# A 64-row score matmul of latent attention, given 128 rows by a zeroed upper half

## The chip, the cores and the metric

The kernel runs on one core of a Trainium2 chip. The metric is the device time of one execution in microseconds (us), the lower the better. Times are medians of several executions. The engines are named as in the profile: PE (TensorE matmul), PEld (TensorE weight load), DVE (VectorE), ACT (ScalarE), POOL (GpSimd) and SP (SyncE, which issues most of the DMAs).

## What is computed

The kernel is one inference step of a two-layer decoder: a prompt of 1024 tokens and 8 new tokens share all weights. Layer 0 mixes with a gated MLP and a convolution, layer 1 with latent attention, and each layer ends in a SwiGLU FFN. The change lies in the prompt's attention in layer 1, which the reference computes so, for each of 8 heads (the nope part of a query or key has 128 features, the rotary part 64, and the rotary key is shared by all heads):

```python
q_nope, q_pe, ckv, kpe = mla_project(h, pos, w_in_c, q_norm, kv_norm, w_uq)
k_nope = jnp.einsum('btr,rhn->bthn', ckv, w_uk)
...
s = (jnp.einsum('bqhn,bkhn->bhqk', qn_b, k_nope)
     + jnp.einsum('bqhp,bkp->bhqk', qp_b, kpe)).astype(jnp.float32) * ATTN_SCALE
...
s = jnp.where(kpos[None, :] <= qpos[:, None], s, -jnp.inf)
p = jax.nn.softmax(s, axis=-1).astype(v.dtype)
return jnp.einsum('bhqk,bkhv->bqhv', p, v)
```

## The kernel before

Everything is float32 in value. For the large products each operand is split into a high and a low part of a type that TensorE multiplies in one pass, and three products are added up in PSUM (high by high, high by low, low by high).

**The rotary part.** The rotary key has 64 features. `KD` (128 rows by 1024 keys) holds the key's high part twice, in rows 0 to 63 and again in rows 64 to 127 (L788, with a DMA at L787 that doubles the rows). `KL` (64 rows) holds the key's low part (L789). The query tile `QS` has 128 rows: the high part of the rotary query above its low part. So the matmul of `QS` with `KD` gives high by high and low by high at once (L1097), and the matmul of the upper 64 rows of `QS` with `KL` gives high by low (L1098).

**The scores.** `scores` (from L1077) goes over the blocks of 128 queries of a chunk; a chunk is three such blocks, or two at the end. Block i sees (i+1) x 128 keys, in pieces of at most 512. A piece is a group of five matmuls into one PSUM tile `mm`: L1094 and L1095 with the stationary `qh`, L1096 with `qlo`, L1097 and L1098 with `QS`. Then DVE adds the mask of the diagonal block (L1100) and takes the maximum (L1101), and ACT takes the exponential (L1103). There are 12 pieces a head and 96 in all: 48 of 512 keys, and 16 each of 128, 256 and 384.

**Work around it.** In each of 24 steps (8 heads by 3 chunks) `weave` mixes the scores of this step with the values of the step before (transposes at L1137, products at L1148 to L1150), the values' preparation (L1047 to L1049) and pieces of the attention of the 8 new tokens (L938, L939, L941, L1001), whose matmuls have outputs of 32 columns and, at L941, 64 rows. The keys of a head are made by `mm3` (L202 to L204) with 512 columns. There are four `mm` and four `aux` tiles in PSUM. The tile framework then fixes one order for each engine; every engine takes its instructions in that order and waits on semaphores. POOL zeroes a mask (L748), issues the DMAs of the rotary key (L785, L787) and, in the attention, gathers the cache pages (L893). SP loads the query tiles (L1075) and the weights (L167).

Of the kernel before, what the change touches and what calls it, by code (L numbers as in the profile page):

```python
# [66 lines left out]

# [1 line left out]
UNITS = []  # L69
# [31 lines left out]

# [1 line left out]
VC = {}  # L103
# [9 lines left out]
def hybrid_step(ctx: ExitStack, tc: tile.TileContext,  # L113
# [11 lines left out]

# [1 line left out]
    ident = const.tile([P, P], F32, name="ident")  # L127
# [28 lines left out]

# [1 line left out]
    WR, WS = 2, 4  # L158
# [35 lines left out]

# [1 line left out]
    class Env:  # L196
# [16 lines left out]
    def auxtile():  # L213
        return env.psum.tile([P, 512], F32, tag="aux", name="aux", bufs=env.naux)
# [21 lines left out]
    def rstd_rows(acc, n, width):  # L236
        """1/sqrt(acc summed over partitions / width + eps), the same on every partition, in PSUM."""
        blocks = [(b, min(P, n - b * P)) for b in range((n + P - 1) // P)]
        pst = auxtile()
        for b, w in blocks:  # L240
            PE.matmul(pst[:w, b:b + 1], acc[:, b * P:b * P + w], ones[:, 0:1], start=True, stop=True)
        r = small()
        full = len([1 for b, w in blocks if w == P])
        ACT.activation(r[:, :full], pst[:, :full], AF.Sqrt, bias=eps_t, scale=1.0 / width)
        if full < len(blocks):
            w = blocks[-1][1]
            ACT.activation(r[:w, full:full + 1], pst[:w, full:full + 1], AF.Sqrt, bias=eps_t[:w], scale=1.0 / width)
        DVE.reciprocal(r[:, :full], r[:, :full])
        if full < len(blocks):
            DVE.reciprocal(r[:w, full:full + 1], r[:w, full:full + 1])  # L250
        dg = tmp()
        for b, w in blocks:
            DVE.tensor_scalar(dg[:w, b * P:b * P + w], ident[:w, :w], r[:w, b:b + 1], None, ALU.mult)
        prs = auxtile()
        for b, w in blocks:
            PE.matmul(prs[:, b * P:b * P + w], ones[:w, :], dg[:w, b * P:b * P + w], start=True, stop=True)  # L256
        return prs
# [10 lines left out]
    def gemm_act(u, c, ps):  # L268
        """128 output features (unit of 8 x 128 columns) x token chunk c."""
        wh, wl = unit(u)  # L270
        c0, n = CH[c]
        for k in range(KT):
            mm3(ps[:, :n], wh[:, k * P:(k + 1) * P], wl[:, k * P:(k + 1) * P],
                ah(k, c0, c0 + n), al(k, c0, c0 + n), k == 0, k == KT - 1)
# [27 lines left out]

    # DRAM scratch
    x_spill = tc.dram_tile([KT, P, T], F32, name="x_spill")
    # scaled queries of every head, in two parts: nope hi, nope lo, rope (hi above lo)
    q_spill = tc.dram_tile([HEADS, 3, P, SEQ], F32, name="q_spill")
# [16 lines left out]

    # ======================= layer 0: even mixer =======================
    with ExitStack() as ph:
# [18 lines left out]

        # w_s[g, 0, 0] times the 8 x 8 identity
        w8 = p1.tile([NB, 4, NB], F32, name="w8")
        for g in range(4):
            DVE.tensor_scalar(w8[:, g, :], ident[:NB, :NB], w00B[:, g:g + 1], None, ALU.mult)

# [1 line left out]
        conv_ops = []  # L351
# [4 lines left out]
        def fma(out, i, a, k, e0, e1):  # L356
            """tap k of channel tile i over the tokens e0..e1-1"""
            r = DVE.scalar_tensor_tensor(out, G[:, i, k + e0:k + e1], cw[:, i, k:k + 1], a[:, e0:e1], ALU.mult, ALU.add)  # L358
            if PIN:
                tc.keep_in_program_order(r)  # L360
# [4 lines left out]
        def conv_early(i0):  # L365
            """the first chunk of tokens, all taps but the last"""
            accs = [cacc(), cacc()]
# [40 lines left out]

# [1 line left out]
        def pair(m, c):  # L410
# [40 lines left out]

# [1 line left out]
        def sample_conv():  # L453
# [17 lines left out]
        if SC == 0:  # L471
            sample_conv()
# [1 line left out]
        NTOK = 9  # L474
# [8 lines left out]
        def v_stats(n, w):  # L483
            """of a tile of tokens: vst[0] = -mean, vst[1] = sum of squares about the mean"""
            mean = vst[:w, 0, n:n + 1]
# [57 lines left out]

# [1 line left out]
        Tbs = {}  # L545
        utiles = {}

        def gate(m, c):
# [3 lines left out]
            if c == 0:  # L552
                Tb = p1.tile([P, P], F32, tag="Tb", name="Tb", bufs=4)
                pr = auxtile()  # row sums of the masked spatial weights, on every partition
                PE.matmul(pr[:, :P], ones, wsT[:, g, :], start=True, stop=True)
                DVE.scalar_tensor_tensor(Tb, pr[:, :P], col("gb", m), bsB[:, g, :], ALU.mult, ALU.add)
                Tbs[m] = Tb
# [39 lines left out]

# [1 line left out]
        def add_x(m, c, ps):  # L599
# [15 lines left out]

# [1 line left out]
        def ln_conv(c):  # L617
# [28 lines left out]

    # ======================= FFN =======================
    def ffn(layer, final):
# [84 lines left out]

    # ======================= layer 1: latent attention =======================
    xstack.close()
# [5 lines left out]
    KD = mp.tile([P, SEQ], F32R, name="KD")  # L741
    KL = mp.tile([64, SEQ], F32R, name="KL")
    qs_n = mp.tile([P, HEADS, NB], F32, name="qs_n")
# [8 lines left out]
    with ExitStack() as ph:  # L752
# [18 lines left out]
        def evac_c(u, c, ps):  # L771
# [7 lines left out]
            else:  # L779
# [8 lines left out]
                ACT.copy(KD[:, c0:c0 + npr], kr[:, :npr])  # L788
                DVE.tensor_tensor(KL[:, c0:c0 + npr], kr[:64, :npr], KD[:64, c0:c0 + npr].bitcast(F32), ALU.subtract)  # L789
                if c == 2:  # L790
# [25 lines left out]

        # queries: tiles 0..7 = nope of a head; 8, 10 = first rope halves of 4 heads; 9, 11 = second halves
        def spill(src, n, hi_to, lo_to, eng):
            """SCALE * src in two parts"""
            th, tl = [env.tmp.tile([P, 512], F32R, tag="t", name="t", bufs=env.ntmp) for _ in range(2)]  # L820
# [44 lines left out]

# [1 line left out]
    acts["pool"].release()  # L867
    with ExitStack() as ph:
# [3 lines left out]
        def sample_attention():  # L872
            """Generator: the attention of the 8 new tokens over their pages, cut into pieces."""
            sp = pa
# [6 lines left out]
            DVE.tensor_copy(idx, pgf[:, :64])  # L881
            # queries in the latent space, 8 heads a token; 32 columns are taken from a token's first one on,
            # and only the first 8 of the rows that come out are used
            ql = sp.tile([P, 2, 88], F32, name="ql")
# [20 lines left out]
            for g in range(4):  # L905
# [10 lines left out]
                if g % 2:  # L916
                    yield
            # the new latent rows, token-major
            cn8 = sp.tile([NB, 256], F32, name="cn8")
# [7 lines left out]
            for r in range(2):  # L927
# [45 lines left out]
                yield  # L973
                # probabilities with the keys on the partitions, then the latent outputs
                ols = sp.tile([P, 256], F32, tag="ols", name="ols", bufs=1)
# [62 lines left out]
        def prep_v(hp):  # L1038
            """values of heads 2hp, 2hp+1, token-major"""
            wh, wl = unit(("uv", hp // 2))  # L1040
# [37 lines left out]
        def scores(h, c, out):  # L1078
            c0, n = CP[c]
            qh, qlo, QS = KQ.pop(("q", h, c))  # L1080
            for i in range(c0 // P, (c0 + n) // P):
# [3 lines left out]
                two = len(pieces) == 2  # L1085
                # -maximum of each piece, sums, factors, then -maximum and 1/sum of the row
                st = pa.tile([P, 8], F32, tag="st", name="st", bufs=6)
                prs = []
                for pi, (a, e) in enumerate(pieces):
# [7 lines left out]
                    PE.matmul(o, QS[:, r], KD[:, a:e], start=False, stop=False, skip_group_check=True)  # L1097
                    PE.matmul(o, QS[:64, r], KL[:, a:e], start=False, stop=True, skip_group_check=True)  # L1098
                    if e == nk:
# [60 lines left out]
        def out_proj_half():  # L1160
            """heads 0..3 through the output projection, added to the residual in DRAM (prompt tokens)"""
            for q in range(4):
# [22 lines left out]
        def weave(gens):  # L1185
            """takes items of several generators in turn, each spread over the whole"""
            lists = gens
# [51 lines left out]
    for c0, n in CH:  # L1239
        for k in range(KT):  # L1240
            (nc.gpsimd if k % 2 < XQ else nc.sync).dma_start(XT[:, k, c0:c0 + n], x_spill[k][:, c0:c0 + n])
# [1 line left out]
    rawp = tc.alloc_tile_pool(name="rawp", bufs=1, reuse_waits="tile")  # L1243
# [38 lines left out]
def _unit_array(u, w):  # L1282
    """One unit of weights, [128 partitions, 1024]: 128 rows of a factor on the partitions."""
    def cols(a, c0, n):
# [125 lines left out]
```

## Time and profile before

| what | value |
|---|---|
| median of 3 executions | 2805.55 us |
| their range | 2802.09 to 2808.86 us |
| span of the profiled execution (first to last instruction) | 2785.5 us |
| PE busy, share of the span | 2732.5 us, 98% |
| PEld busy | 2615.7 us, 94% |
| DVE, ACT, POOL busy | 1437.2, 751.2, 206.7 us |
| granted TensorE clock, mean | 0.993 of full speed |

The profile gives the span of the profiled execution and no total of its own. The median of the three timed executions is 20.05 us above that span; this is what lies around it (the launch and the end). A busy share of 98% on PE counts every matmul from its start to its modelled end, and the ends overlap the next start. What one matmul really takes from the stream is the distance from its start to the start of the next one.

### The profile page before, as it was taken

The page shows a single profiled execution, that of the slowest core. Times are in us where ns is not written, and L with a number is a line of the kernel's source. Part 1 is how long each engine was busy: PE and PEld are TensorE (multiplying, and loading weights), DVE is VectorE, ACT ScalarE, POOL GpSimd, SP SyncE. Part 2 cuts the span into 40 slices and gives each one's busy share as a digit, 9 for nine tenths or more (in the row PEclk, how much of TensorE's full clock was granted, in tenths as well). Part 3 has the DMA queues.
Part 4 walks back from the last instruction along what each step waited for, and adds up shares of the span by engine and source line. Part 5 has one row for each costly group of instructions (what it writes and reads, how often), then busy time and mean ns, then how long its engine had stood idle before and what let it go on. Part 6 is the DMA issues. An engine that isn't in the chain of part 4 may idle for free.

```text
span 2785.5 us, 41891 instructions
## 1 busy us (share of the span) xinstructions
PE 2732.5 (98%) x17434; PEld 2615.7 (94%) x17434; DVE 1437.2 (52%) x2716; ACT 751.2 (27%) x1562; POOL 206.7 (7%) x293
## 2 busy tenths in 40 slices
PE   7999999999999999999997999999999999999998
PEld 7999999999999999999996867967999999999998
DVE  8999889765232323232754557457652323232325
ACT  5112531542212121212342435235422121212122
POOL 0000010000000000000101144243100000000000
PEclk9999999999999999999998999999999999999999
DMA  3111122112111111111313644442211111111111
GB/s 117 62 47 47 48 70 68 60 33 67 46 52 48 46 46 46 46 46 46 115 60 125 227 125 122 157 131 88 100 61 42 50 52 47 46 46 46 46 46 61
DMA packets 79949, 197.29 MB, mean 71 GB/s; under 512 B 11824, under 2 KB 41712, under 8 KB 79760
## 3 DMA queue, kind: packets, MB, share of 16 engines
q1 hardware_dynamic: 64816, 152.85, 16.7%
q0 software_dynamic: 14944, 41.78, 4.8%
q8 instruction: 136, 2.23, 0.3%
q14 instruction: 53, 0.43, 0.0%
HBM read 166.57 MB, written 27.74 MB: 70 GB/s over the span
## 4 chain that ended last, share of the span: by engine, by line
PE 77%; DMA 2%; DVE 1%; ACT 0%; issue 0%; SPq 0%; DVEq 0%; ACTq 0%
PE mm L202 22%; PE mm L204 21%; PE mm L203 21%; DMA q_spill<-t 2%; PE aux L1137 1%; PE mm L1098 1%; PE mm L1094 1%; PE mm L1095 1%; PE aux L938 1%; PE aux L941 1%; PE mm L1148 1%; PE mm L1149 1%; PE mm L1097 1%; PE mm L1096 1%; PE mm L1150 1%; PE aux L256 1%
## 5 line engine op out<-in xcount | busy, mean ns | idle before, releaser
L202 PE MATMUL mm<-act_hia,whi 128*128 128x384 f32 (+2 forms) x1812 | 582.6, 322 | 3.5 <-ACT cz L775 1.3
L204 PE MATMUL mm<-act_hia,wlo 128*128 128x384 f32 (+2 forms) x1812 | 580.2, 321 | 1.0 <-DVE wlo L181 1.0
L203 PE MATMUL mm<-act_loa,whi 128*128 128x384 f32 (+2 forms) x1812 | 581.1, 321 | 0.0
L202 PE MATMUL mm<-act_hib,whi 128*128 128x384 f32 (+1 forms) x1620 | 520.4, 321 | 0.0
L204 PE MATMUL mm<-act_hib,wlo 128*128 128x384 f32 (+1 forms) x1620 | 519.8, 321 | 0.0
L203 PE MATMUL mm<-act_lob,whi 128*128 128x384 f32 (+1 forms) x1620 | 517.7, 320 | 0.0
L180 ACT CAST whi<-wraw 128x1024 fp32r<-128x1024 f32 x205 | 214.9, 1049 | 716.3 <-PE mm L203 608.4
L663 DVE TENSOR_TENSOR t<-mm,t 128x384 f32<-128x384 f32 x132 | 68.1, 516 | 571.7 <-PE mm L204 570.7
L202 PEld LDWEIGHTS mm<-act_hia,whi 128*128 128x128 f32 x1812 | 341.3, 189 | 5.5 <-ACT act_hia L207 2.0
L204 PEld LDWEIGHTS mm<-act_hia,wlo 128*128 128x128 f32 x1812 | 341.3, 188 | 1.3 <-DVE wlo L181 1.2
L203 PEld LDWEIGHTS mm<-act_loa,whi 128*128 128x128 f32 x1812 | 341.4, 188 | 0.9 <-DVE act_loa L208 0.6
L202 PE MATMUL mm<-hh,whi 128*128 128x384 f32 (+1 forms) x1056 | 338.5, 321 | 0.0
L204 PE MATMUL mm<-hh,wlo 128*128 128x384 f32 (+1 forms) x1056 | 337.6, 320 | 0.0
L203 PE MATMUL mm<-hl,whi 128*128 128x384 f32 (+1 forms) x1056 | 337.3, 319 | 0.0
L181 DVE TENSOR_TENSOR wlo<-wraw,whi 128x1024 fp32r<-128x1024 f32 x205 | 250.0, 1224 | 163.9 <-ACT whi L180 163.8
L203 PEld LDWEIGHTS mm<-act_lob,whi 128*128 128x128 f32 x1620 | 305.1, 188 | 0.1
L202 PEld LDWEIGHTS mm<-act_hib,whi 128*128 128x128 f32 x1620 | 305.1, 188 | 0.1
L204 PEld LDWEIGHTS mm<-act_hib,wlo 128*128 128x128 f32 x1620 | 304.6, 188 | 0.0
L358 DVE SCALAR_TENSOR_TENSOR cacc<-G,cw,cacc 128x1024 f32<-128x1024 f32 (+2 forms) x290 | 290.5, 1065 | 0.0
L697 DVE TENSOR_TENSOR XT<-mm,XT 128x384 f32<-128x384 f32 (+1 forms) x288 | 147.9, 515 | 232.7 <-PE mm L204 232.0
L203 PEld LDWEIGHTS mm<-hl,whi 128*128 128x128 f32 x1056 | 199.0, 188 | 0.0
L202 PEld LDWEIGHTS mm<-hh,whi 128*128 128x128 f32 x1056 | 198.6, 188 | 0.0
(330 smaller groups left out, 3413.6 us busy)
## 6 DMA issues: line engine op xcount, KB each, us to landing
wraw<-in_W SPq DMA_DIRECT2D x205, 512.0 KB
q_spill<-t SPq DMA_DIRECT2D x48, 192.0 KB
XT<-in_xT SPq DMA_DIRECT2D x16, 192.0 KB
XT<-in_xT POOLq DMA_DIRECT2D x16, 192.0 KB, 2.9
x_spill<-XT POOLq DMA_DIRECT2D x16, 192.0 KB, 2.2
q_spill<-t SPq DMA_DIRECT2D x24, 128.0 KB
qh<-q_spill SPq DMA_DIRECT2D x16, 192.0 KB
qs<-q_spill SPq DMA_DIRECT2D x16, 192.0 KB
```

Source lines behind the costliest of these rows:

```text
L180: ACT.copy(hi, raw)
L181: DVE.tensor_tensor(lo, raw, hi.bitcast(F32), ALU.subtract)
L202: PE.matmul(ps, wh, ah, start=first, stop=False, skip_group_check=True)
L203: PE.matmul(ps, wh, al, start=False, stop=False, skip_group_check=True)
L204: PE.matmul(ps, wl, ah, start=False, stop=last, skip_group_check=True)
L256: PE.matmul(prs[:, b * P:b * P + w], ones[:w, :], dg[:w, b * P:b * P + w], start=True, stop=True)
L358: r = DVE.scalar_tensor_tensor(out, G[:, i, k + e0:k + e1], cw[:, i, k:k + 1], a[:, e0:e1], ALU.mult, ALU.add)
L663: DVE.tensor_tensor(sg[:, :n], pu[:, :n], sg[:, :n], ALU.mult)
L697: DVE.tensor_tensor(XT[:, m, c0:c0 + n], ps[:, :n], XT[:, m, c0:c0 + n], ALU.add)
L938: PE.matmul(o, ql[:, 0, 8 * b:8 * b + 32], kt_[:, 0:P], start=True, stop=False, tile_position=tp)
L941: PE.matmul(o, qp[:, 8 * b:8 * b + 32], kt_[:64, 2 * P:3 * P], start=False, stop=True, tile_position=tp)
L1094: PE.matmul(o, qh[:, r], kh[:, :w], start=True, stop=False, skip_group_check=True)
```

## The change

`KL` gets 128 rows. POOL sets rows 64 to 127 to zero once, right after the tile is made, DVE writes the low part into rows 0 to 63 as before, and the fifth matmul of a piece takes all 128 rows of `QS` and `KL`. The lower half of `QS` (the low part of the query) meets the zeros. Nothing else in the program differs but comments. In the changed kernel all lines behind the new one stand one line further down (L1098 becomes L1099).

```diff
     KD = mp.tile([P, SEQ], F32R, name="KD")
-    KL = mp.tile([64, SEQ], F32R, name="KL")
+    KL = mp.tile([P, SEQ], F32R, name="KL")
+    nc.gpsimd.memset(KL[64:, :].bitcast(F32), 0.0)
...
-                DVE.tensor_tensor(KL[:, c0:c0 + npr], kr[:64, :npr], KD[:64, c0:c0 + npr].bitcast(F32), ALU.subtract)
+                DVE.tensor_tensor(KL[:64, c0:c0 + npr], kr[:64, :npr], KD[:64, c0:c0 + npr].bitcast(F32), ALU.subtract)
...
                     PE.matmul(o, QS[:, r], KD[:, a:e], start=False, stop=False, skip_group_check=True)
-                    PE.matmul(o, QS[:64, r], KL[:, a:e], start=False, stop=True, skip_group_check=True)
+                    PE.matmul(o, QS[:, r], KL[:, a:e], start=False, stop=True, skip_group_check=True)
```

The order of PE, DVE, ACT and SP is the same instruction for instruction. POOL has one instruction more. This is POOL's row around it, before, from the end of layer 0 (`x_spill` stores the residual) to the DMAs of the rotary key:

```order
L722 DMA x_spill<-XT 128x264 x8
L748 MEMSET dmask 128x128
L749 AFFINE_SELECT dmask<-dmask 128x128
L785 DMA out_kpe<-t 64x384
L787 DMA t<-t 64x384
```

And after:

```order
L722 DMA x_spill<-XT 128x264 x8
L743 MEMSET KL 64x1024
L749 MEMSET dmask 128x128
L750 AFFINE_SELECT dmask<-dmask 128x128
L786 DMA out_kpe<-t 64x384
L788 DMA t<-t 64x384
```

The memset stands ahead of the mask's; nothing else moved. On PE, in the first step of the attention, the first matmul with `KL` in the changed kernel waits for POOL, where it waited for nothing:

```order
L1096 MATMUL mm<-kl,qh 128x128 [waits DVE_49]
L1097 MATMUL mm<-kh,ql__13841 128x128 [waits DMAHW7_49]
L1098 MATMUL mm<-KD,qs 128x128 [waits DMAHW0_49]
L1099 MATMUL mm<-KL,qs 128x128 [waits Pool_49]
L1096 MATMUL mm<-kl,qh 128x256
L1097 MATMUL mm<-kh,ql__13841 128x256
L1098 MATMUL mm<-KD,qs 128x256
L1099 MATMUL mm<-KL,qs 128x256
```

It is the only one of the 96 that has this wait; the others follow without one.

## Rows read from the trace of the kernel before

**Rows 1.** The page: the span, and busy us of each engine.

```profile
span 2785.5 us, 41891 instructions
PE 2732.5 (98%) x17434; PEld 2615.7 (94%) x17434; DVE 1437.2 (52%) x2716; ACT 751.2 (27%) x1562; POOL 206.7 (7%) x293
```

**Rows 2.** Attention stretch: length, PE, PEld, DVE, ACT, POOL busy, clock, DMA share, GB/s.

```profile
1571.00:1955.00 384.00, 382.56 (x2342) 287.06 (x2343) 241.36 (x742) 154.01 (x454) 140.00 (x160) 0.99 0.42 129
```

**Rows 3.** Instructions of L1098: min/median/max ns, first and last start, forms.

```profile
L1098 PE MATMUL mm<-KL,qs x96: 323/491/687, 1573.1 to 1952.7; 64*128 64x512 f32 x48, 64*128 64x128 f32 x16, 64*128 64x256 f32 x16, 64*128 64x384 f32 x16
```

**Rows 4.** Timeline of PE, pieces of 512: start us, us, line, rows*columns, moving operand.

```profile
1582.51 0.39 PE L1096 MATMUL mm<-kh,ql__13896 128*128 128x512 f32 x1
1582.74 0.40 PE L1097 MATMUL mm<-KD,qs 128*128 128x512 f32 x1
1583.06 0.49 PE L1098 MATMUL mm<-KL,qs 64*128 64x512 f32 x1
1583.48 0.50 PE L1094 MATMUL mm<-kh,qh 128*128 128x512 f32 x1
1583.82 0.39 PE L1095 MATMUL mm<-kl,qh 128*128 128x512 f32 x1
```

**Rows 5.** Timeline of PE, three pieces of 128, 256 and 384.

```profile
1709.13 0.33 PE L1095 MATMUL mm<-kl,qh 128*128 128x128 f32 x1
1709.30 0.28 PE L1096 MATMUL mm<-kh,ql__15417 128*128 128x128 f32 x1
1709.41 0.28 PE L1097 MATMUL mm<-KD,qs 128*128 128x128 f32 x1
1709.61 0.33 PE L1098 MATMUL mm<-KL,qs 64*128 64x128 f32 x1
1709.87 0.38 PE L1095 MATMUL mm<-kl,qh 128*128 128x256 f32 x1
1710.09 0.28 PE L1096 MATMUL mm<-kh,ql__15417 128*128 128x256 f32 x1
1710.21 0.28 PE L1097 MATMUL mm<-KD,qs 128*128 128x256 f32 x1
1710.42 0.38 PE L1098 MATMUL mm<-KL,qs 64*128 64x256 f32 x1
1710.73 0.44 PE L1095 MATMUL mm<-kl,qh 128*128 128x384 f32 x1
1711.01 0.34 PE L1096 MATMUL mm<-kh,ql__15417 128*128 128x384 f32 x1
1711.18 0.34 PE L1097 MATMUL mm<-KD,qs 128*128 128x384 f32 x1
1711.45 0.44 PE L1098 MATMUL mm<-KL,qs 64*128 64x384 f32 x1
1711.82 0.42 PE L1001 MATMUL aux<-kt,pq 128*32 128x256 f32 x3
```

**Rows 6.** Timeline of PEld: the weight loads of the first of these pieces.

```profile
1709.35 0.19 PEld L1097 LDWEIGHTS mm<-KD,qs 128*128 128x128 f32 x1
1709.61 0.18 PEld L1098 LDWEIGHTS mm<-KL,qs 64*128 64x128 f32 x1
```

**Rows 7.** Waits of PEld, 1560 to 1990: us in total, times, longest.

```profile
PEld mm L1098 <- issue: 20.9, 62, 0.4
PEld aux L941 <- issue: 12.7, 64, 0.2
...
PEld mm L1094 <- ACT kh L207: 1.8, 7, 0.3
```

**Rows 8.** Timeline of POOL: the idle time ahead of the first rotary-key DMA.

```profile
1442.37 0.59 POOL L785 DMA_DIRECT2D out_kpe<-t  x1 [43.78 <-PE mm L204]
```

**Rows 9.** Groups by line, POOL: the largest memset, busy us, mean ns, idle before.

```profile
L343 POOL MEMSET G<- 128x240 f32 x1 | 0.3, 289 | 0.0
```

**Rows 10.** Busy us by engine, columns as in rows 2: DVE's densest ten microseconds.

```profile
1690.00:1700.00 10.00, 10.00 (x62) 7.35 (x62) 9.43 (x30) 6.74 (x22) 0.76 (x1) 1.00 0.34 111
```

## The prediction, made before the changed kernel ran

> **What bounds the kernel now.** I read the page first: PE is busy in 98% of the span, and no other engine is above 52% [rows 1]. So the end of the kernel moves with PE's stream, and I go to the one stretch that the change touches, the attention from 1571 to 1955 us. There PE is busy in 382.56 of 384 us, while DVE has 241.36 and ACT 154.01 [rows 2]. PE hardly ever stands still. But "busy" does not say that it streams: a matmul counts from its start to its modelled end, and these overlap. The view that tells is the timeline of PE, read by the distance from one start to the next. In a run of full tiles that distance depends only on the width: 0.23 us for 512 columns (L1096 to L1097, [rows 4]), 0.17 for 384, 0.12 for 256 and 0.11 for 128 (the same pair, [rows 5]).
>
> Around the 64-row matmul with `KL` this rule breaks, three times in each piece. **Entering**: from L1097 to L1098 it takes 0.32 instead of 0.23 at 512 [rows 4], 0.27 instead of 0.17 at 384, 0.21 instead of 0.12 at 256, and 0.20 instead of 0.11 at 128 [rows 5]. **Leaving**: from L1098 to whatever follows it takes 0.42, 0.37, 0.31 and 0.26 us, where the widths ask for 0.23, 0.17, 0.12 and 0.11. **The matmul after that**: the first full matmul behind `KL` holds the stream for 0.34 at 512 (1583.48 to 1583.82, [rows 4]), 0.28 at 384 and 0.22 at 256 [rows 5], about 0.11 too long. At 128 the nearest row is L1095 at 1709.13, which follows a tile of 32 columns and takes 0.17, 0.06 too long.
>
> Why: PEld shows it. `KD`'s weights start to load at 1709.35, while the matmul before it (1709.30, 0.28 long) still runs. `KL`'s weights start at 1709.61, at the very time of their matmul; nothing was loaded ahead [rows 5, 6]. The loads themselves are equally long, 0.19 and 0.18 us. The wait list puts 62 stops of L1098's loads, 20.9 us, down to "issue", that is, to no other engine. The other matmul with 64 rows, L941 of the new tokens, has 64 such stops [rows 7]. So I read it as the price of changing the shape of the tile (rows by columns) between neighbours: into 64*128, and back out.
>
> **The change part by part.** The order of PE, DVE, ACT and SP is the same in both programs, so the sum is made on PE's stream, by pieces. There are 48 of 512 and 16 each of the others [rows 3].
> *Entering and leaving.* At 512: 0.09 + 0.19 = 0.28, times 48 = 13.4 us. At 384: 0.10 + 0.20 = 0.30, times 16 = 4.8. At 256: 0.09 + 0.19 = 0.28, times 16 = 4.5. At 128: 0.09 + 0.15 = 0.24, times 16 = 3.8. Together 26.5 us.
> *Where the next one has a narrow shape anyway.* I counted 12 of the 96 pieces whose follower is a matmul of the new tokens (the last row of [rows 5] is one). There a change of shape remains behind a full `KL`; it should cost what entering costs now, 0.09. This takes 12 x 0.09 = 1.1 off: 25.4 us.
> *The matmul after.* In the other 84 pieces the follower is full. 25 of these are transposes of 128 columns and 4 are 128-wide score matmuls: 29 x 0.06 = 1.7 us. The other 55 save 0.11 each, 6.0 us. Together 7.7. That a transpose gains here is the softest of the terms; if the whole item gives nothing, 25.4 us stay, and with it the sum is 33.1 us. I take 33, since the excess stands plainly in the rows for the full score matmuls.
> *The matmul itself.* With 128 rows it streams the same columns; the full matmuls of the same width show the 0.23 us that I have set. The load has the same 128 columns. Cost: nothing.
> *The memset.* One more POOL instruction, 1024 columns. The nearest row is a memset of 240 columns in 0.289 us [rows 9]; scaled by columns it is 1.2 us. Behind it on POOL stand the mask's memset and select and the DMAs of the rotary key. POOL is idle for 43.78 us ahead of the first of these [rows 8], and that idle time hides it. Without that cover it would cost its 1.2 us once. It cannot gain anything, since it replaces nothing.
> *The new wait.* One PE instruction, the first matmul with `KL` at 1573.1 [rows 3], now waits for POOL. The memset has its place before 1442.37, some 130 us earlier, so this costs nothing. Behind that matmul all of PE would be queued, but it has been released long before.
> *What is late next.* PE's stretch goes from 384 to about 351 us. DVE's 241.36 us become 69% of it instead of 63%, ACT's 154.01 become 44%. On average there is room. But in its densest ten microseconds DVE is busy for 9.43 [rows 10], and if PE covers the same work in 9.1, DVE falls behind by 0.3 us there. PE also has waits on ACT and DVE that are short now, of which the commonest is on `kh`, 7 times, 1.8 us [rows 7]. Each such place can take back at most what was saved since the last one, about 0.35 us (0.28 and part of 0.11). From that wait list I count some 35 places, so at most 12 us come back; at least nothing does. I take 3, near the low end, because PE's 1.4 us of idle time in the stretch say that the others are ahead now [rows 2].
>
> **Sum.** 33 - 3 = 30 us. The profiled span goes from 2785.5 to 2755.5 us. What lies around the span stays as it was, 20.05 us to the median of the runs shown, 2805.55. So I forecast 2775.5 us.
>
> **The rivals.**
> *The others hand it back.* PE reaches its waits on `kh`, on the transposed probabilities and on free `mm` tiles too early, and DVE and ACT set the pace in the dense steps. For it: 9.43 of 10 us on DVE [rows 10]. Against it: only one stretch is that dense, and DVE has 143 us to spare in the whole [rows 2]. With 12 us back from a saving of 25 to 33 there stay 13 to 21 us: 2785 to 2793.
> *It does not do what it says.* The stops belong to something that the change keeps, such as loading the same `QS` twice in a row, or the last matmul of an accumulation. Then the time stays at 2805.5. Against it: leaving costs most, and there the next stationary is another one; L941 stops in the same way with weights of its own [rows 7]. The rows show a lone 64-row matmul that takes longer than a full one. The Trainium skill states another result ("TensorE: Matmul & The Clock Gate", section "Why this matters for your kernels", small-K row): a single matmul with few rows takes the same time as one with 128, and the gain lies only in running several at once; by that rule the sum would be zero, and the trace does not bear it out, with 0.42 against 0.23 us [rows 4].
> *Slower: the load no longer hides.* If the full-height load of `KL` could not run beside the full-height matmul with `KD`, its 0.19 us would stand open: 0.23 + 0.19 = 0.42 at 512 where entering takes 0.32 now, so 0.10 more, and 0.09 to 0.10 more at the other widths. Leaving would cost the same again, as now. That is 96 x 0.10 = 9.6 us more: 2815. It decides as soon as more than 0.09 us of a load is open and leaving gains nothing. Against it: `KD`'s load, of just this shape, does start during the full matmul before it [rows 6]. The same page of the Trainium skill, section "Part 3: Packing small matmuls — row/col tiling", says that a weight load overlaps a running matmul only where the two lie in different row groups, which would make this rival the forecast; the load at 1709.35 contradicts it.
>
> **How the numbers follow.** The forecast (24 to 36 us gained) gets 0.79, the handing back 0.15, no effect 0.04, slower 0.02. The range begins at the whole 33 us, less about 4 for the scatter of the runs shown (2802.09 to 2808.86): 2768. It ends at the upper end of the handing back, 2792. Faster means more than 0.2% (5.6 us), about what a measurement of this kernel can tell from no change. Forecast and handing back both lie beyond it, 0.94; within it 0.04; slower 0.02.
>
> **What would show it.** Right: L1099 appears as 128*128, with a median near that of the `KD` matmul instead of 491 ns; its loads start during the matmul ahead and have no "issue" stops; the distances 0.32, 0.42 and 0.34 at 512 all become 0.23; the attention ends about 30 us sooner and the rest keeps its length. Handing back shows as longer waits of L1094 on `kh` or of the transposes on DVE. Wrong: distances around L1099 that stay above the width's, or loads that open between `KD` and `KL`.

## The result, and the profile after

The changed kernel takes 2771.57 us (2769.67 to 2772.35), the kernel before 2805.84 us beside it: a ratio of 0.9881, with a 95% interval of 0.9869 to 0.9893. That is 34 us less, inside the range and 4 us below the forecast.

One number of the profile before was misread. The time of an execution and its span lie about 2 us apart in every later execution, of either kernel (1.7 to 2.8; 2771.33 and 2769.4 us for the trace below). So the 2785.5 us of [rows 1] belong to an execution of about 2787 us and not to one of 2805.55, and 20 us never lay around the span. Chips differ: later runs of the same kernel before gave medians of 2787 us on one chip and 2801 us on another. Ratios are therefore taken on one chip only, and lengths of stretches are compared only between traces of one chip.

The page of the changed kernel, first line and busy times:

```profile
span 2769.4 us, 41892 instructions
PE 2705.9 (98%) x17434; PEld 2616.6 (94%) x17434; DVE 1433.9 (52%) x2716; ACT 750.4 (27%) x1562; POOL 208.0 (8%) x294
```

The timeline of PE, a piece of 512 as in [rows 4], now with L1099 for the `KL` matmul (start us, us, line, rows*columns, moving operand):

```profile
1578.94 0.39 PE L1097 MATMUL mm<-kh,ql__13897 128*128 128x512 f32 x1
1579.18 0.39 PE L1098 MATMUL mm<-KD,qs 128*128 128x512 f32 x1
1579.41 0.39 PE L1099 MATMUL mm<-KL,qs 128*128 128x512 f32 x1
1579.64 0.40 PE L1095 MATMUL mm<-kh,qh 128*128 128x512 f32 x1
1579.87 0.40 PE L1096 MATMUL mm<-kl,qh 128*128 128x512 f32 x1
```

The distances are 0.24, 0.23, 0.23 and 0.23 us, where they were 0.23, 0.32, 0.42 and 0.34. The narrow pieces, as in [rows 5], from a second trace of the changed kernel (run e9_after):

```profile
1695.84 0.27 PE L1098 MATMUL mm<-KD,qs 128*128 128x128 f32 x1
1695.95 0.28 PE L1099 MATMUL mm<-KL,qs 128*128 128x128 f32 x1
1696.06 0.33 PE L1096 MATMUL mm<-kl,qh 128*128 128x256 f32 x1
1696.23 0.28 PE L1097 MATMUL mm<-kh,ql__15418 128*128 128x256 f32 x1
1696.35 0.28 PE L1098 MATMUL mm<-KD,qs 128*128 128x256 f32 x1
1696.47 0.28 PE L1099 MATMUL mm<-KL,qs 128*128 128x256 f32 x1
1696.59 0.34 PE L1096 MATMUL mm<-kl,qh 128*128 128x384 f32 x1
...
1696.94 0.34 PE L1098 MATMUL mm<-KD,qs 128*128 128x384 f32 x1
1697.12 0.34 PE L1099 MATMUL mm<-KL,qs 128*128 128x384 f32 x1
1697.39 0.63 PE L1002 MATMUL aux<-kt,pq 128*32 128x256 f32 x6
```

At 128 and 256 entering and leaving now take 0.11 and 0.12 us. At 384 entering takes 0.18; leaving takes 0.27, because the follower has 32 columns and so still changes the shape: 0.09 too long, as reckoned for the 12 pieces of this kind.

The weight loads around L1099 in the first trace, to be held against [rows 6]:

```profile
1578.95 0.19 PEld L1098 LDWEIGHTS mm<-KD,qs 128*128 128x128 f32 x1
1579.18 0.19 PEld L1099 LDWEIGHTS mm<-KL,qs 128*128 128x128 f32 x1
1579.41 0.19 PEld L1095 LDWEIGHTS mm<-kh,qh 128*128 128x128 f32 x1
```

`KL`'s load starts at 1579.18, with the `KD` matmul, and is over before its own matmul starts at 1579.41. The instructions of L1099 (min/median/max ns, first and last start, forms) answer to [rows 3], and POOL's timeline to [rows 8, 9]:

```profile
L1099 PE MATMUL mm<-KL,qs x96: 272/388/628, 1572.5 to 1938.0; 128*128 128x512 f32 x48, 128*128 128x128 f32 x16, 128*128 128x256 f32 x16, 128*128 128x384 f32 x16
```

```profile
1398.49 0.95 POOL L743 MEMSET KL<- 64x1024 f32 x1 [17.96 <-ACT act_hib L207]
...
1442.63 0.59 POOL L786 DMA_DIRECT2D out_kpe<-t  x1 [42.56 <-PE mm L204]
```

The median of the matmul went from 491 to 388 ns; that of the `KD` matmul ahead of it is 389. The memset took 0.95 us and ended 43 us ahead of the DMA that stands behind it.

### The profile page after: what moved, and what is told of

Its sections match the earlier page's. It is cut to its first block, busy times and chain, and to the rows that moved or that the text cites. A ratio compares the mean times of both kernels' runs of the same rounds, so it can differ in the third digit from the quotient of the medians.

```text
span 2769.4 us, 41892 instructions
## 1 busy us (share of the span) xinstructions
PE 2705.9 (98%) x17434; PEld 2616.6 (94%) x17434; DVE 1433.9 (52%) x2716; ACT 750.4 (27%) x1562; POOL 208.0 (8%) x294
## 4 chain that ended last, share of the span: by engine, by line
PE 77%; DMA 2%; DVE 1%; issue 1%; ACT 0%; DVEq 0%; SPq 0%; ACTq 0%
PE mm L202 22%; PE mm L204 22%; PE mm L203 22%; DMA q_spill<-t 2%; PE aux L1138 1%; PE aux L939 1%; PE aux L942 1%; PE mm L1095 1%; PE mm L1150 1%; PE mm L1149 1%; PE mm L1099 1%; PE mm L1096 1%; PE mm L1151 1%; PE mm L1097 1%; PE mm L1098 1%; PE aux L256 1%
```

## The experiments

**The kernel before once more, and the changed one beside it** (chip with 2787 us for before). No edit.

> The kernel before once more, unchanged, to get the span that belongs to its own time. The first profile has a span of 2785.5 us while the timed runs have a median of 2805.8; in the changed kernel span and time are 1.9 us apart (2769.4 and 2771.3). Theory A (the profiled execution of before was an unusually quick one): the span of this run lies 1.9 us under its time, near 2804, and the attention is longer than the 384 us of the first profile by up to 18 us. Theory B (before has 20 us around its span that the change took away): the span is again near 2785 with a time near 2805.

> The changed kernel once more. Ratio to before 0.988. The first profile showed 13.2 us of idle PE in the attention (355.8 busy of 369), against 1.4 in before. If the other engines hand that back steadily, the same places stall again (about 13 us); if they are chance events of one execution, the places and the sum differ.

Before: 2787.77 us, ratio 1.0003 (0.9993 to 1.0014), profiled at 2786.93 us with a span of 2785.0. Of the two theories on the 20 us the first one is nearer, but the other way round: an execution with a span of 2785 us is an ordinary one on this chip. The timed runs of the first comparison then came from a slower chip; this is inferred, since nothing tells on which chip the first trace was taken. Changed: 2754.14 us, ratio 0.9883 (0.9867 to 0.9900), 33.1 us less, as on the first chip. The attention of both, in busy us by engine (length, PE, PEld, DVE, ACT, POOL, clock, DMA share, GB/s), before and after:

```profile
1571.00:1955.00 384.00, 383.29 (x2338) 287.70 (x2339) 240.29 (x738) 153.26 (x452) 141.04 (x160) 0.99 0.42 128
```

```profile
1571.00:1924.00 353.00, 351.72 (x2347) 286.94 (x2346) 237.46 (x743) 153.12 (x455) 140.53 (x160) 0.99 0.45 141
```

The same work now fits into 353 us, and PE is idle for 1.3 us of it against 0.7. The 13.2 us of idle PE in the first trace of the changed kernel are absent here.

**The tile without the matmul.** The tile of 128 rows and its memset stay, the matmul is as before:

```diff
-PE.matmul(o, QS[:, r], KL[:, a:e], ...)
+PE.matmul(o, QS[:64, r], KL[:64, a:e], ...)
```

> The tile of 128 rows and its memset stay, the matmul with KL goes back to 64 rows. Theory (the shape of the matmul is the whole cause): ratio 1.000 to before, the distances 0.32, 0.42 and 0.34 us back. Rival (the memset or another place of the tile in SBUF did it): ratio 0.988.

Measured: 2785.2 us, ratio 0.9998 (0.9988 to 1.0008), and in its trace the distances at 512 are 0.32, 0.42 and 0.34 again (means over the pieces). Neither the memset, nor its place in POOL's queue, nor the taller tile moves the time. The matmul's own shape is the whole cause.

**The 64 rows one place earlier.** The changed kernel, with `KD`'s matmul cut to 64 rows:

```diff
-PE.matmul(o, QS[:, r], KD[:, a:e], ...)
+PE.matmul(o, QS[:64, r], KD[:64, a:e], ...)
```

This leaves out a product of the scores, the query's low part with the key's high part.

> The changed kernel with the fourth matmul of a piece (KD) cut to 64 rows, which leaves out the product of the query's low part with the key's high part; KL stays at 128. Theory (a change of shape between neighbours costs, wherever it stands): ratio about 1.000, since each piece again goes into 64 rows and back; 0.32 us from L1097 to the KD matmul and 0.42 from it to KL at 512, 0.34 for KL. Rival (the stop belongs to the last matmul of a group or to loading QS twice): ratio 0.988, as the changed kernel.

Measured: 2789.86 us, ratio 1.0012 (1.0003 to 1.0022). The whole gain is gone. Its timeline of PE at a piece of 512:

```profile
1581.12 0.40 PE L1097 MATMUL mm<-kh,ql__13897 128*128 128x512 f32 x1
1581.44 0.50 PE L1098 MATMUL mm<-KD,qs 64*128 64x512 f32 x1
1581.87 0.50 PE L1099 MATMUL mm<-KL,qs 128*128 128x512 f32 x1
1582.21 0.28 PE L1048 MATMUL mm<-whi,kv_hi 128*128 128x256 f32 x1
```

0.32 into the 64-row matmul, 0.43 out of it, 0.34 for the full one behind. These are the three distances of [rows 4], moved by one place. The last matmul of the group is now L1099 and takes only what every first full matmul behind a change takes. So neither the end of a group nor the second load of `QS` is what stops.

**Two 64-row matmuls side by side.** The kernel before, with the same cut of `KD`, so that `KD` and `KL` both have 64 rows.

> The kernel before with both matmuls of the rotary part, KD and KL, at 64 rows; this leaves out the product of the query's low part with the key's high part. Theory (only a change of shape between neighbours costs): as many changes as before, so ratio 1.000; 0.23 us from KD to KL at 512, 0.32 into KD, 0.42 out of KL. Rival (each 64-row matmul is slow by itself): 96 more of them at 0.19 to 0.28 us, 18 to 27 us more, ratio 1.007 to 1.010.

Measured: 2807.66 us, ratio 1.0027 (1.0011 to 1.0043), on a chip where before takes 2801 us: between the two theories, nearer the first. It was run again where before takes 2787.55 us.

> KD and KL both at 64 rows (the product of the query's low part with the key's high part is left out), beside before on one chip. It came out at 1.0027 where equal counts of changes ask for 1.000. By the distances of its trace (0.33 into KD, 0.34 from KD to KL, 0.32 out of KL at 512, against 0.23, 0.33 and 0.42) about 2 us more than before are due, ratio 1.001; if 64 rows cost something of their own, 1.003 again and the excess shows in a distance.

Measured: 2790.77 us, ratio 1.0009 (0.9999 to 1.0018). So 96 more 64-row matmuls cost next to nothing while they change no shape. The 7 us more of the chip with 2801 us are open; there is no trace of before from it. The timeline of PE (run e10_two64) corrects the picture, for my distances for `KD` to `KL` and out of `KL` were wrong:

```profile
1581.25 0.40 PE L1096 MATMUL mm<-kh,ql__13896 128*128 128x512 f32 x1
1581.58 0.50 PE L1097 MATMUL mm<-KD,qs 64*128 64x512 f32 x1
1581.92 0.39 PE L1098 MATMUL mm<-KL,qs 64*128 64x512 f32 x1
1582.23 0.50 PE L1094 MATMUL mm<-kh,qh 128*128 128x512 f32 x1
1582.57 0.40 PE L1095 MATMUL mm<-kl,qh 128*128 128x512 f32 x1
```

0.33 into `KD`, 0.34 from it to `KL`, 0.31 out of `KL`, 0.34 for the next. Each change has two parts: about 0.09 us ahead of the first matmul in the new shape, and about 0.11 us on that matmul itself. A lone 64-row matmul is the first of its shape and has a change behind it, so 0.23 + 0.11 + 0.09 = 0.43 are due and 0.42 to 0.43 measured, and the full one behind it pays 0.11 again. Two changes, 0.39 us a piece at 512.

**Half the dose.** The changed kernel, with 128 rows for the pieces of 512 alone:

```diff
+kr_ = P if w == 512 else 64
-PE.matmul(o, QS[:, r], KL[:, a:e], ...)
+PE.matmul(o, QS[:kr_, r], KL[:kr_, a:e], ...)
```

> The changed kernel with 128 rows only for the 48 pieces of 512 keys; the other 48 go back to 64 rows. By the terms (entering 0.09, leaving 0.18, the matmul after 0.10 where it is full) 48 pieces save about 17 us of the 32: ratio 0.994. If the gain hung on something that happens once, such as a schedule that shifts, it would be 0.988 or 1.000.

Measured: 2780.41 us against 2801.06, ratio 0.9937 (0.9917 to 0.9958). Half the pieces give about half the gain: it is a sum of single prices, not one event.

**The same step for the new tokens.** In the changed kernel, the rotary query of the new tokens gets 128 rows too, the upper 64 zero; the cache pages are already padded with zeros there:

```diff
-qp = sp.tile([64, 88], F32, name="qp")
+qp = sp.tile([P, 88], F32, name="qp")
...
-PE.matmul(o, qp[:, 8 * b:8 * b + 32], kt_[:64, 2 * P:3 * P], ...)
+PE.matmul(o, qp[:, 8 * b:8 * b + 32], kt_[:, 2 * P:3 * P], ...)
...
```

> The changed kernel, and the same step for the rotary matmul of the new tokens (L942, 64 rows by 32 columns): the query tile qp gets 128 rows with zeros above, and the cache page's rows, which are already padded with zeros in memory, are taken whole. Its 64 matmuls stand between others of 128 rows by 32 columns. In the trace they take 0.31 us to enter and 0.33 to leave where two passes of the full height take 0.24: 64 x (0.07 + 0.09) = 10 us, ratio about 0.9845 to before. Rival (the change of columns, which stays, is what costs there): 0.988.

Measured: 2750.52 us, ratio 0.9826 (0.9806 to 0.9846), on the chip where before takes 2801 us. The 0.9845 of ten microseconds lies at the very end of that interval. Then on one chip with before and after:

> The kernel before, for a trace from the same chip as the next three. Ratio 1.000. Theory A (where a chip is slower, it is slower by stalls at fixed places of the attention, whatever the kernel): if this chip gives about 2800 us, the PE stalls of the changed kernel's first trace (near 1584 and 1903 to 1910 us, 13 us in sum) show here too; if it gives about 2787 us, they do not. Theory B (those stalls came from the change, as other engines handing time back): they are absent here at any speed of the chip.

> The changed kernel beside it. Ratio 0.988. Theory A: the idle time of PE in the attention is that of e8_before to about 2 us. Theory B: it is 10 us or more above it.

> The changed kernel with the new tokens' rotary matmul at full height too, beside the changed kernel on one chip. 0.9826 to before was measured, about 16 us better than the changed kernel, where two changes of shape for each of 64 matmuls gave 10. If the rest comes from the four column tiles that now follow each other in one shape and run at the same time, their starts lie 0.03 us apart and the loads of L939 stop at 10 places instead of 59; ratio 0.983, and 0.994 to e9_after.

Measured: before 2789.28 us, ratio 0.9999 (0.9989 to 1.0008); changed 2754.25 us, 0.9877 (0.9861 to 0.9894); with the new tokens' matmul 2721.07 us, **0.9758** (0.9742 to 0.9775). This version beats both, and by 33 us instead of 10: the term was mis-sized by a factor of three. The busy time of PE in all matmuls of the cache pages (columns: length, PE, PEld, POOL busy, clock, DMA share, GB/s) shows where it comes from, in e9_after and then in e11_qp128:

```profile
1571.00:1924.00 353.00, 69.95 (x512) 33.91 (x512) 123.50 (x128) 1.00 0.46 142
```

```profile
1571.00:1892.00 321.00, 37.78 (x512) 23.74 (x512) 122.49 (x128) 0.99 0.50 156
```

69.95 - 37.78 = 32.2 us, as much as the span gains (2752.5 to 2720.9). The timelines of PE tell how, e9_after first. These operands are float32 and a matmul takes two passes (x2):

```profile
1624.15 0.41 PE L939 MATMUL aux<-kt,ql 128*32 128x128 f32 x2
1624.39 0.38 PE L940 MATMUL aux<-kt,ql 128*32 128x128 f32 x2
1624.70 0.40 PE L942 MATMUL aux<-kt,qp 64*32 64x128 f32 x2
1625.04 0.41 PE L939 MATMUL aux<-kt,ql 128*32 128x128 f32 x2
```

```profile
1620.36 0.27 PE L940 MATMUL aux<-kt,ql 128*32 128x128 f32 x1
1620.37 0.30 PE L939 MATMUL aux<-kt,ql 128*32 128x128 f32 x1
1620.47 0.27 PE L940 MATMUL aux<-kt,ql 128*32 128x128 f32 x1
1620.50 0.27 PE L939 MATMUL aux<-kt,ql 128*32 128x128 f32 x1
1620.58 0.27 PE L942 MATMUL aux<-kt,qp 128*32 128x128 f32 x1
1620.61 0.27 PE L940 MATMUL aux<-kt,ql 128*32 128x128 f32 x1
```

With the 64-row matmul between them, one token's three matmuls run one after the other, 0.89 us a token. In one shape throughout, the matmuls of different tokens, which have different 32 columns of the array, run at the same time: an L940 of one token and an L939 of the next start 0.01 us apart. The change of shape had kept them apart. By the distances, three matmuls of two passes in one shape but one after the other would take 3 x 0.24 = 0.72 us a token, 11 us less for the 64; the other 21 us come from running side by side. This split is an estimate; no run separates the two.

## Why the prediction was right, step by step

**The stream of PE.** The mechanism held: `KL`'s loads have no "issue" stop any more (20.8 us before, in e8_before; L1099 is absent from the list of e9_after), and all three distances fell. The forecast for the stream was 33.1 us; 33.1 were measured on the chip of the second comparison (2787.20 to 2754.14 us). That the two agree to the last digit is luck, since single executions of before scatter from 2781 to 2792 us. By terms, from the mean distances in e1_before and e2_after: *entering* (the 94 pieces in which `KL` follows `KD` directly) went from 0.325 to 0.233 us at 512, 0.279 to 0.186 at 384, 0.219 to 0.125 at 256 and 0.207 to 0.121 at 128. Times 48 and 16 this is 8.8 us, forecast 8.8. *Leaving* went from 0.424 to 0.243, 0.386 to 0.224, 0.323 to 0.125 and 0.254 to 0.119: 16.6 us, forecast 16.7 with the 12 narrow followers taken off. *The matmul after* gave 6.7 us, forecast 7.7. The transposes, called the softest part, gave 1.4 of 1.5; the other full followers 5.3 of 6.2. What was missed there are the 16 followers of the 128-key pieces: a wider matmul behind one of 128 columns takes 0.05 too long even in one shape (1696.06 to 1696.23 above, 0.17 at 256 instead of 0.12), and the prediction had read its 0.11 at 256 from such a row. All else in the attention sums to 0.1 us. From the first to the last matmul of L1094 (then L1095) it took 381.25 us and then 349.45, 31.8 less; what is left to 33.1 lies outside it and in the scatter of the executions.

**What comes back.** This term was mis-sized: 3 us were forecast, and on the chip with 2787 us nothing to speak of came back. The waits of the weight loads on `kh`, first in the kernel before and then in the changed one (runs e8_before and e9_after: us in total, times, longest), are the same to the last digit:

```profile
PEld mm L1094 <- ACT kh L207: 1.8, 7, 0.3
```

```profile
PEld mm L1095 <- ACT kh L207: 1.8, 7, 0.3
```

One wait of PE did grow, that of the first `KD` matmul on the query's DMA:

```profile
PE mm L1097 <- DMA qs<-q_spill: 0.2, 1, 0.2
```

```profile
PE mm L1098 <- DMA qs<-q_spill: 1.0, 1, 1.0
```

That is 0.8 us, once. DVE's densest stretch [rows 10] held nobody up, since its lag is shorter than what the PSUM tiles bridge. This last clause is argued, not tested.

**Memset and new wait.** 1.2 us was the estimate, 0.95 measured; hidden, as the tile-only run shows at 0.9998.

**The span's surroundings.** The 20.05 us were no constant of the launch. The sum went right because it was a difference.

**The rivals.** That the change does nothing is out, and so is the open load: `KL`'s load starts with `KD`'s matmul. The two statements of the Trainium skill weighed there ("TensorE: Matmul & The Clock Gate") do not describe this stream: a lone 64-row matmul costs 0.39 us more than a full one at 512, neighbours included, and full-height loads do run beside full-height matmuls. For loads the same section also names an exception, the background weight buffer, which the prediction left out. Another page of the Trainium skill fits: "TensorEngine Tiling (Array Packing)", section "Key Properties", says that a change of the tiling mode drains TensorE. The traces agree in that every change of shape holds the stream up; that it is a drain they do not show. The page gives no price, and here it is about 0.2 us a change.

**Handing back.** It looked true at first: the first trace of the changed kernel has 13.2 us of idle PE in the attention (13.0 from the first piece to the last). Its largest stop stands at the same place as one in e4_two64, whose matmuls are slower than before's, both on chips where before takes over 2800 us:

```profile
1587.62 0.79 PE L1095 MATMUL mm<-kh,qh 128*128 128x512 f32 x1 [3.98 <-issue]
```

```profile
1588.76 0.50 PE L1094 MATMUL mm<-kh,qh 128*128 128x512 f32 x1 [1.79 <-issue]
```

On the chip with 2787 us neither before nor after has a stop there (e8_before, e9_after). So these stops need no faster PE, only such a chip. But they grow with a faster PE. Four traces come from chips where before takes over 2800 us, and all four stop at this matmul. The attention in them, from the first to the last piece, the longest first (e4_two64, e6_only512, the first trace of the changed kernel, e7_qp128; columns as in [rows 2]):

```profile
1573.00:1967.30 394.30, 388.10 (x2321) 283.69 (x2321) 240.31 (x737) 152.15 (x450) 140.76 (x160) 0.97 0.40 123
1572.00:1945.30 373.30, 364.45 (x2323) 287.35 (x2324) 237.53 (x731) 150.28 (x448) 140.97 (x160) 0.99 0.42 130
1572.50:1938.00 365.50, 352.52 (x2323) 284.58 (x2323) 235.84 (x731) 149.97 (x447) 140.78 (x160) 0.99 0.43 133
1575.00:1917.00 342.00, 324.20 (x2328) 275.88 (x2329) 235.57 (x733) 151.28 (x450) 140.76 (x160) 0.99 0.46 143
```

PE is idle for 6.2, 8.9, 13.0 and 17.8 us, the more the shorter its stream; on the chip with 2787 us it is about 0.5 us from the first piece to the last for every kernel, e11_qp128 included. So on the slower chips a faster PE does meet longer stops. For this change the ratio is all the same (0.9881 there, 0.9883 on the other chip), so the kernel before should lose about as much there; this is inferred, since it has no trace from such a chip, and the 34 us of the first comparison can't be added up from PE's stream as the 33 us of the second can. With the still shorter stream of the new tokens' version more is lost: 0.9826 there and 0.9758 on the other chip. What causes the stops stays open.

## What to carry to other kernels

Read PE by the distance from start to start, not by its busy time: 98% busy hid 32 us in the attention. Where a matmul has fewer rows or columns than its neighbours, look whether its weights load ahead; if not, and if zeros can fill the rows at no cost, make the shapes equal, or put the odd ones side by side. Take a span and a time from one execution before calling their difference a constant.

## What the runs showed of the hardware

- A change of the tile's rows from 128 to 64 or back costs PE about 0.20 us in this stream: 0.09 ahead of the first matmul in the new shape and 0.11 on that matmul (0.06 where it has 128 columns to stream). A second matmul in the new shape pays neither (e10_two64). The part ahead is the same for a change of columns (0.27 instead of 0.18 into 128*32).
- Equal shapes at different columns run at the same time, starts 0.01 us apart; one matmul of another height between them ends that. Without it the matmuls of the cache pages take 32 of 70 us less.
- Chips differ by up to 19 us in 2800 for the same kernel. The ratio of this change is nearly the same (0.9881 on a slower chip, 0.9883 and 0.9877 on the chip with 2787 us), but that of the new tokens' version is not (0.9826 and 0.9758).
